# Product 7 of Strassen's scheme as a block product over two groups, in a matmul with RMSNorm

## The chip, the cores and the metric

The kernel runs on one core of one Trainium2 chip. The metric is the device time of an execution in microseconds; three runs of the kernel before gave 220.73 (median), 220.69 and 220.97. A core has TensorE (matmuls, into PSUM), VectorE, ScalarE and GpSimd (called POOL in the profile), and SyncE (SP), which here only issues DMAs. Each engine works through its own instructions in the order of the program; semaphores tie them together.

## The reference

```python
m, k, n = 2048, 2048, 2048          # all float32, eps = 1e-5
x = np.matmul(a, b)
rms = np.sqrt(np.mean(x ** 2, axis=-1, keepdims=True) + eps)
return gamma * x / rms
```

## The kernel before

The 2048 rows of `a` are 16 row blocks of 128 rows (`mb` 0 to 15). Blocks 0 to 3 are the head: their product runs while `b` streams in, partly as plain matmuls (L388). From then on the 2048x2048 matrix `b` stays in SBUF as bf16, in two halves `j` of N, each as eight tiles `raw[j][kp]`.

**Groups.** Blocks 4 to 15 are six groups `g` = 2 to 7 of two blocks, `ra` = 2g and `rb` = 2g+1. For a group and a half `j`, the 2x2 block product (two row blocks, two column chunks of 512, K taken as pairs of 128) is done by Strassen's seven products; each is eight matmuls of 128x128 by 128x512 into one PSUM bank (`product`, L289, matmul at L285). The sums of quarters of `b` were made in the head (`b_sums`, and `b_sums_in_place`, L273, which adds the diagonal quarters to the off-diagonal ones). The sums of quarters of `a` are five tiles `s_1`, `s_2`, `s_5`, `s_6`, `s_7` (`a_sums`, L254, each one 128x1024 fp16 operation on VectorE at L260), overwritten for each group. Product 7 is (a12 - a22), which is `s_7`, times the in-place quarter `b_quarter(j, kp, 1, 0)`.

**A half of a group** is `group_half` (L582). TensorE's order is products 2, 5, 1, 4, 3, 7, 6; products 4 and 3 add into the banks of 2 and 5 after those have been copied out. ScalarE copies banks into the x tiles (`c` at L597, `x21` at L608, `x12` at L613) and squares finished chunks with a running sum (`square`, L299; `last_squares`, L573, takes those that VectorE finished last). VectorE makes the differences and sums (L601, L605, L610, L615, L619, L624). The chunk `x22` also serves as scratch `t` and `c`, so it is the first x tile that a half writes (L597). PSUM has seven banks for this, in rotation.

**Work around it** is put in by hand at eight points of a half, `hooks` 0 to 7 (`hooks_of`, L634): point 1 lies after the first product, 2 after the second, 3 after product 1, 4 after product 4, 5 after product 3, 6 after product 7, 7 after product 6. In the first half (`j` = 0) of a group the two blocks of the next group are prepared: `row_norm` (L214, two squares on ScalarE at L219), `row_factor` (L225, four small VectorE operations), `row_apply` (L236: ScalarE scales the fp32 row block to fp16, L242) and `transpose_dma` (L194: SP issues a DMA transpose out of the fp16 rows, L195). The fp16 rows lie in two slots of `head_at` (`a16_slot`, L80). Also in the first half, block 2g-2 is scaled by gamma and 1/rms (`scale`, L363, on VectorE at L370) at point 3 and stored at point 4 (`store`, L374, SP at L376), behind the transpose that point 4 issues. In the second half, point 2 finishes block 2g-1 (`finish`, L378: scale and store of each half row), points 3, 6 and 7 make the next group's sums, and at point 0 POOL waits for the first half's `x22` (`wait_for`, L125, and `load_after`, L628) and then loads two row blocks (L121) into the two buffers `a32`.

**x tiles.** Each row block's result is two fp32 tiles of 128x1024; eight slots `x_slot` go round (`x_tile`, L313), four for a group.

**The last group** is `last_group` (L705), with its own order: products 5, 1, 4, 3, 7 for both halves, then 2 and 6, the very last in two quarters (L800), and the end of the normalization.

Of the kernel before, what the change touches and what calls it, by code (L numbers as in the profile page):

```python
# [17 lines left out]
def kernel(  # L18
# [21 lines left out]
    CH = 512  # L40
# [39 lines left out]
    def a16_slot(mb):  # L80
        if mb == HB:
            return gamma_sb[:, 0:HALF].bitcast(FP16)
        flat = head_at.rearrange("p t r m -> p (t r m)").bitcast(FP16)
        return flat[:, (2 + mb % 2) * K:(3 + mb % 2) * K]

    s_sum = {s: consts.tile([P, KP, P], FP16, name=f"s_{s}") for s in (1, 2, 5, 6, 7)}

    def at(mb):
# [161 lines left out]

    def sum_of(g, s):
        return s_sum[s].bitcast(BF16) if g < G0 else s_sum[s]

# [42 lines left out]
    x_half = {}  # L296
    n_x = [0]

# [7 lines left out]
    def square_half(mb, h):  # L306
# [4 lines left out]
                             scale=inv_sqrt_n, accum_out=msq[mb][:, c:c + 1])  # L311

    def x_tile(mb, h):  # L313


        if (mb, h) not in x_half:
            n = n_x[0]
            n_x[0] += 1
            if n < 8:
                slot = n  # L320
            else:
                g = n // 4
                slot = ((0, 4, 1, 5), (0, 1, 4, 5))[g // 2 % 2 == 0][n % 4] + 2 * (g % 2)
            x_half[mb, h] = x_slot[slot]
        return x_half[mb, h]
# [256 lines left out]
    def group_half(g, j, hooks):  # L582
# [21 lines left out]
        product(g, j, 1, p1)  # L604
        nc.vector.tensor_tensor(out=t, in0=p1, in1=t, op=ALU.subtract)  # L605
        at_hook(3)
        product(g, j, 4, p2, start=False)
        nc.scalar.copy(out=x21, in_=p2)  # L608
        square(rb, x21)
        nc.vector.tensor_tensor(out=x11, in0=t, in1=x21, op=ALU.add)  # L610
        at_hook(4)
# [4 lines left out]
        at_hook(5)  # L616
        p7 = new_bank()
        product(g, j, 7, p7)
        nc.vector.tensor_tensor(out=x11, in0=p7, in1=x11, op=ALU.add)  # L619
        late.append((ra, x11))  # L620
        at_hook(6)
# [3 lines left out]
        late.append((rb, x22))  # L625
        at_hook(7)

    def load_after(g, mb):  # L628
# [5 lines left out]
    def hooks_of(g, j):  # L634
# [13 lines left out]
        if j == 0:  # L648
            if g == G0:
                hook(0, finish, 0, (1,))  # L650
                hook(1, row_norm, nxt)
                hook(1, take_rms, 1)
                hook(2, pair_sub)
                hook(2, row_factor, nxt)
                hook(2, apply, nxt)
                hook(2, row_norm, nxt + 1)
                hook(2, pair_sums)
                hook(2, a_sums, g, (7, 6))
                hook(2, finish, 0, (0,))
                hook(2, finish, 1, (1,))  # L660
                hook(2, row_factor, nxt + 1)
                hook(2, pair_ends)
                hook(2, scale, 1, (0,))
                hook(4, apply, nxt + 1)
                hook(4, store, 1, (0,))
                hook(7, late.insert, 0, (r2, None))
            else:
                done = [2 * g - 2, 2 * g - 1]
                if g == G0 + 1:
                    done.insert(0, r3)  # L670
                else:
                    hook(1, row_norm, nxt)
                for mb in done:
                    hook(1, take_rms, mb)
                hook(2, row_factor, nxt)
                hook(2, apply, nxt)
                if g == G0 + 1:
                    hook(2, finish, r3)
                hook(2, row_norm, nxt + 1)
                hook(3, scale, 2 * g - 2)  # L680
                hook(3, row_factor, nxt + 1)
                hook(4, apply, nxt + 1)
                hook(4, store, 2 * g - 2)
        else:
# [4 lines left out]
            else:  # L689
                hook(2, finish, 2 * g - 1)  # L690
            if more:
                hook(3, a_sums, g + 1, (2, 5, 1))
                hook(6, a_sums, g + 1, (7,))
                hook(7, a_sums, g + 1, (6,))
# [10 lines left out]
    def last_group():  # L705
# [35 lines left out]
        for j in range(2):  # L741
# [3 lines left out]
            nc.scalar.copy(out=t[j], in_=p5)  # L745
            last_squares()
            product(g, j, 1, p1)
            add(t[j], p1, t[j], ALU.subtract)
            if j == 0:
                finish(2 * g - 2)  # L750
            product(g, j, 4, p4[j])
            nc.scalar.copy(out=x21[j], in_=p4[j])
            add(x11[j], t[j], x21[j])
            if j == 0:
                finish(2 * g - 1)
            product(g, j, 3, p5, start=False)
            nc.scalar.copy(out=x12[j], in_=p5)
            square(ra, x12[j])
            add(t[j], x11[j], x12[j])
            p7 = new_bank()  # L760
            product(g, j, 7, p7)
            add(x11[j], p7, x11[j])
            square(ra, x11[j])
            if j == 0:
                product(g, j, 2, p4[j], start=False)
                nc.scalar.copy(out=x21[j], in_=p4[j])
                square(rb, x21[j])
                seed = p7
                add(seed, t[j], x21[j], ALU.subtract)
# [5 lines left out]
        halves = [slice(0, CH // 2), slice(CH // 2, CH)]  # L775
        half = [bank[:, 0:CH // 2] for bank in (p1, p7)]
        for bank, col in zip(half, halves):
# [77 lines left out]
```

## Time and profile before

| | |
|---|---|
| median of three runs (lowest, highest) | 220.73 us (220.69, 220.97) |
| profiled execution: span, first to last instruction | 219.1 us; the runs' median is 1.6 us above it, for what lies around the span |
| TensorE matmul (PE) | 209.2 us busy, 95%, 1032 instructions |
| VectorE (DVE) | 165.9 us, 76%, 326 |
| ScalarE (ACT) | 127.0 us, 58%, 263 |
| GpSimd (POOL) | 36.4 us, 17%, 75 |
| granted TensorE clock over the span | 0.994 |
| matmuls of the groups (L285) | start at 41.20 us, without a pause from 66.73 us |
| stores to `out` | 29 of 512 KB, median 3.7 us from issue to landing |
| loads of row blocks | 10 of 1024 KB, median 9.0 us |
| DMA transposes of row blocks | 10, median 4.3 us |

How to read it: each engine's busy time is added up over the whole span. The profile gives, for each group of instructions, the source line, engine, operation, tiles, shapes and count, then busy time and the mean duration of one in ns, then the idle time of the engine just before them and what ended it. The chain that ended last is followed back from the last instruction; its shares tell which engine's work sets the end. In a timeline, each row is a start and a length in us, and the bracket at its end gives the idle time before and its releaser. "SPq" is SP's queue, "PEclk" the TensorE clock that was granted, as a fraction of full speed.

### The profile page before, as it was taken

How to read it: one execution, taken by the hardware profiler on the slowest of the kernel's cores; microseconds unless marked ns; L12 is line 12 of the kernel's file. 1: busy time of each engine (PE TensorE's matmuls, PEld its weight loads, DVE VectorE, ACT ScalarE, POOL GpSimd, SP SyncE). 2: the span in 40 equal slices, each digit the busy share in tenths (PEclk: the TensorE clock that was granted, in tenths of full speed). 3: DMA queues.
4: the chain of work that ended last, by engine and by line, in shares of the span. 5: the costliest groups of instructions: out<-in, count | busy, mean ns of one | idle time of the engine just before them, and what ended most of it. 6: DMA issues, size and time to landing. Idle time of an engine off the chain costs nothing.

```text
span 219.1 us, 3041 instructions
## 1 busy us (share of the span) xinstructions
PE 209.2 (95%) x1032; PEld 97.7 (45%) x1032; DVE 165.9 (76%) x326; ACT 127.0 (58%) x263; POOL 36.4 (17%) x75
## 2 busy tenths in 40 slices
PE   7799999999999999999999999999999999999970
PEld 3344544444455444444444444444444444444440
DVE  1128899999989998969696639946795759787771
ACT  2110002930599898588945996289747996334471
POOL 7554443433020002200110002000200000000040
PEclk9999999999999999999999999999999999999997
DMA  7999999999929698946799149955699259145045
GB/s 156 168 202 206 204 206 209 212 208 228 407 77 330 243 276 218 349 188 165 212 320 399 64 88 271 350 244 96 160 298 400 37 106 361 79 167 219 1 170 215
DMA packets 36720, 46.60 MB, mean 213 GB/s; under 512 B 22240, under 2 KB 26336, under 8 KB 35424
## 3 DMA queue, kind: packets, MB, share of 16 engines
q0 software_dynamic: 10608, 23.86, 44.1%
q1 hardware_dynamic: 25824, 22.29, 33.7%
q10 hardware_dynamic: 272, 0.26, 0.3%
q8 instruction: 8, 0.13, 0.2%
q14 instruction: 8, 0.07, 0.1%
HBM read 34.60 MB, written 16.78 MB: 234 GB/s over the span
## 4 chain that ended last, share of the span: by engine, by line
PE 92%; DMA 3%; ACT 1%; POOL 1%; issue 1%; DVE 0%; ACTq 0%; POOLq 0%
PE acc L285 71%; PE acc L388 16%; DMA early<-in_a_dram 3%; PE tbank L419 2%; PE tbank L168 2%; PE acc L800 1%; POOL b L102 0%; PE acc L185 0%; PE tbank L185 0%; ACT a L738 0%; DVE head_at L173 0%; ACTq L850 0%; ACT sq L803 0%; ACT rms L352 0%; POOL t_left masks.py:199 0%
## 5 line engine op out<-in xcount | busy, mean ns | idle before, releaser
L285 PE MATMUL acc<-b,s 128*128 128x512 bf16 x408 | 93.3, 379 | 0.0
L285 PEld LDWEIGHTS <-s 128*128 128x128 f16 (+1 forms) x512 | 50.0, 98 | 59.6 <-DVE s L260 0.2
L388 PE MATMUL acc<-b,head_at 128*128 128x512 bf16 x176 | 43.0, 379 | 1.2 <-DMA b<-in_b_dram 0.8
L303 ACT ACTIVATE sq<-x 128x512 bf16<-128x512 f32 x53 | 33.4, 630 | 6.9 <-DVE x L731 3.0
L370 DVE SCALAR_TENSOR_TENSOR x<-x,r,gamma_sb 128x1024 f32<-128x1024 f32 x28 | 34.9, 1282 | 0.7
L219 ACT ACTIVATE sq<-a 128x1024 bf16<-128x1024 f32 x24 | 25.3, 1054 | 3.2 <-DMA a<-in_a_dram 2.5
L388 PEld LDWEIGHTS <-head_at 128*128 128x128 bf16 x176 | 16.9, 97 | 20.4 <-issue 1.3
L242 ACT ACTIVATE head_at<-a,s 128x2048 f16<-128x2048 f32 x10 | 20.0, 1996 | 3.3 <-DVE s L229 3.3
L102 POOL DMA_DIRECT2D b<-in_b_dram x32 | 17.2, 541 | 20.6 <-DMA b<-in_b_dram 14.2
L430 ACT COPY x<-acc 128x512 f32<-128x512 f32 x5 | 2.9, 582 | 24.6 <-PE acc L388 24.6
L285 PEld LDWEIGHTS <-head_at 128*128 128x128 f16 (+1 forms) x112 | 10.9, 98 | 13.2
L285 PE MATMUL acc<-early,head_at 128*128 128x512 bf16 x64 | 14.5, 379 | 0.0
L285 PEld LDWEIGHTS <-at_even 128*128 128x128 f16 x96 | 9.4, 98 | 11.3
L285 PE MATMUL acc<-early,s 128*128 128x512 bf16 x56 | 14.2, 379 | 0.0
L260 DVE TENSOR_TENSOR s<-head_at 128x1024 f16<-128x1024 f16 (+5 forms) x22 | 13.4, 635 | 0.1
L615 DVE TENSOR_TENSOR x<-x,x 128x512 f32<-128x512 f32 x9 | 6.2, 693 | 8.8 <-ACT x L613 8.3
L127 POOL COPY pace<-x 128x1 f32<-128x1 f32 x4 | 1.7, 413 | 66.2 <-DVE x L624 64.9
L597 ACT COPY x<-acc 128x512 f32<-128x512 f32 x9 | 5.2, 573 | 11.5 <-PE acc L285 11.5
L173 DVE COPY head_at<-tbank 128x1024 bf16<-128x1024 bf16 x7 | 4.8, 692 | 8.6 <-PE tbank L168 8.5
L285 PE MATMUL acc<-t_left,s 128*128 128x512 bf16 x48 | 11.3, 379 | 0.0
L783 POOL TENSOR_SCALAR x<-x,r 128x512 f32<-128x512 f32 x1 | 2.7, 2657 | 51.2 <-DVE r L346 51.2
L276 DVE TENSOR_TENSOR b<-b 128x1024 bf16<-128x1024 bf16 x16 | 10.8, 686 | 0.2
(112 smaller groups left out, 238.0 us busy)
## 6 DMA issues: line engine op xcount, KB each, us to landing
out_dram<-x SPq DMA_DIRECT2D x29, 512.0 KB, 3.7
a<-in_a_dram POOLq DMA_DIRECT2D x10, 1024.0 KB, 9.0
b<-in_b_dram POOLq DMA_DIRECT2D x32, 256.0 KB, 10.0
a<-in_a_dram POOLq DMA_DIRECT2D x4, 512.0 KB, 9.8
early<-in_a_dram POOLq DMA_DIRECT2D x7, 256.0 KB, 10.0
gamma_sb<-in_gamma_dram POOLq DMA_DIRECT2D x2, 512.0 KB, 8.4
out_dram<-x SPq DMA_DIRECT2D x3, 256.0 KB, 2.6
out_dram<-a SPq DMA_DIRECT2D x1, 768.0 KB, 3.3
```

Of the source, the lines that this page charges most:

```text
L102: nc.gpsimd.dma_start(out=raw[j][kp][:, t, :], in_=b[lo:lo + P, j * HALF:(j + 1) * HALF])
L173: nc.vector.tensor_copy(out=head_at[:, 2 * kp:2 * kp + 2, :, :], in_=view)
L219: nc.scalar.activation(out=junk, in_=a32[mb][:, h * HALF:(h + 1) * HALF], func=ACTF.Square, scale=2.0 ** -8, accum_out=n2[:, h:h + 1])
L242: nc.scalar.activation(out=a16[mb], in_=a32.pop(mb), func=ACTF.Copy, scale=factor.pop(mb))
L260: nc.vector.tensor_tensor(out=sum_of(g, s)[:, lo:hi, :], in0=x[:, lo:hi, :], in1=y[:, lo:hi, :], op=op)
L276: nc.vector.tensor_tensor(out=flat[:, 1:3, :], in0=flat[:, 1:3, :], in1=flat[:, 0::3, :], op=ALU.add)
L285: nc.tensor.matmul(bank, lhsT[:, kp, :], rhs, start=(start and kp == 0), stop=(kp == KP - 1), skip_group_check=not start)
L303: nc.scalar.activation(out=sq[:, 0:CH], in_=src, func=ACTF.Square, scale=inv_sqrt_n, accum_out=msq[mb][:, c:c + 1])
L370: nc.vector.scalar_tensor_tensor(out=x, in0=x, scalar=inverse_of[mb], in1=gamma_sb[:, h * HALF:(h + 1) * HALF], op0=ALU.mult, op1=ALU.mult)
L388: nc.tensor.matmul(bank, head_at[:, kt, r, :], head_rhs(c, kt), start=(kt == 0), stop=(kt == KT - 1))
L597: nc.scalar.copy(out=c, in_=one[1])
L615: nc.vector.tensor_tensor(out=t, in0=t, in1=x12, op=ALU.add)
```

## The change

From group 4 on, two groups form a pair: 4 with 5, and 6 with 7. Product 7 of both groups and both halves of N is then one 2x2 block product: the rows are the two groups' `s_7`, the columns the two halves `j`, and K is cut in two halves of four `kp`. It is done by seven block products of four matmuls each, 28 matmuls in all for 4 x 8 = 32 before (`sevenths`).

- The first group of a pair leaves product 7 out of both halves, the second too. The seven parts run in three steps: `one` (parts 1 and 7) at point 6 of the first group's second half, `two` (parts 6, 2, 5, 4) at its point 7, `three` (part 3) at point 1 of the second group's first half. For the last group, step `three` follows its first product.
- The z sums, of quarters of `b`: four for each of four k, each 128x512 bf16 on VectorE, made once, in group 4: three for each k at points 4 to 7 of the first half, the fourth for all k at point 1 of the second. One is in place, two go to a region of `head_at`, and the fourth to `x_slot[3]`, which from then on holds no result rows.
- The y sums, of halves of the two groups' `s_7`: four operations of 128x512 fp16 on VectorE for each pair. They use `s_1` and half of `s_6` as room, so sums 1 and 6 of the second group are made in that group's own first half. The second group's `s_7` has a place of its own.
- Partial results pass from bank to bank by a ScalarE copy (`seed`), twice for a pair. The result chunks of the product are added to `x11` of both groups by VectorE; for the second group they are put there first (one by a ScalarE copy), and `t` and `x21` are added in two operations for one.
- The second group finishes block 2g-1 first and 2g-2 later, since 2g-2 is complete only after step `three`.
- The fp16 rows of blocks 6 to 15 are written in place, into the front half of their fp32 buffer `a32`.
- The x slots are a written-out table over the seven that are left.

```diff
     def a16_slot(mb):
         if mb == HB:
             return gamma_sb[:, 0:HALF].bitcast(FP16)
-        flat = head_at.rearrange("p t r m -> p (t r m)").bitcast(FP16)
-        return flat[:, (2 + mb % 2) * K:(3 + mb % 2) * K]
+        if mb == HB + 1:
+            return head_at.rearrange("p t r m -> p (t r m)").bitcast(FP16)[:, 3 * K:4 * K]
+        return a32[mb].bitcast(FP16)[:, 0:K]
...
+    z_sum = {3: z_store[:, 0], 2: z_store[:, 1],
+             4: x_slot[3].bitcast(BF16).rearrange("p (k n) -> p k n", k=KQ)}
+    s7_second = spare[1].bitcast(FP16).rearrange("p (k m) -> p k m", k=KP)
+    y_sum = {3: s_sum[1][:, 0:KQ], 2: s_sum[1][:, KQ:], 4: s_sum[6][:, 0:KQ]}
...
+    slot_of = {(r, h): r + HB * h for r in range(HB) for h in range(2)}
+
+    for n, slots in enumerate(((0, 4, 1, 5), (2, 6, 3, 7), (0, 1, 4, 5), (2, 7, 6, 1),
+                               (0, 5, 4, 2), (6, 1, 7, 5))):
+        for m, slot in enumerate(slots):
+            slot_of[HB + 2 * n + m % 2, m // 2] = slot
...
         nc.vector.tensor_tensor(out=t, in0=p1, in1=t, op=ALU.subtract)
+        if second_of_pair(g):
+            nc.vector.tensor_tensor(out=x11, in0=x11, in1=t, op=ALU.add)
         at_hook(3)
...
-        p7 = new_bank()
-        product(g, j, 7, p7)
-        nc.vector.tensor_tensor(out=x11, in0=p7, in1=x11, op=ALU.add)
-        late.append((ra, x11))
+        if g < FIRST_PAIR:
+            p7 = new_bank()
+            product(g, j, 7, p7)
...
+    def sevenths(g):
...
+        def one():
+            part(1, 1, y11, lambda k: z11[k], start=True)
+            part(7, 7, y_sum[3], lambda k: z_sum[3][:, k, :], start=True)
+            seed(2, 1)
+            nc.scalar.copy(out=to21, in_=b[7])
+
+        def two():
+            part(6, 2, y_sum[2], lambda k: z_sum[2][:, k, :])
+            part(2, 1, y12, lambda k: z21[k])
+            seed(3, 2)
+            add(to11, 1)
+            square(2 * g, to11)
+            part(5, 3, y21, lambda k: z12[k])
+            nc.vector.tensor_tensor(out=to22, in0=b[3], in1=to21, op=ALU.add)
+            part(4, 2, y22, lambda k: z_sum[4][:, k, :])
+            add(to21, 2)
+
+        def three():
+            part(3, 3, y_sum[4], lambda k: z22[k])
+            add(to12, 3)
+            square(2 * g, to12)
...
                 done = [2 * g - 2, 2 * g - 1]
+                if second_of_pair(g):
+                    done.reverse()
+                    hook(1, a_sums, g, (1,))
+                    hook(1, steps[g - 1][2])
+                    hook(2, a_sums, g, (6,))
...
+            if g == FIRST_PAIR:
+                for k in range(KQ):
+                    hook(1, z_sums, k, (3,))
+            if first_of_pair(g):
+                steps[g] = sevenths(g)
+                hook(3, a_sums, g + 1, (2, 5, 7))
+                hook(4, y_sums, g, (3, 1, 2))
+                hook(6, steps[g][0])
+                hook(7, y_sums, g, (4,))
+                hook(7, steps[g][1])
+            elif more:
                 hook(3, a_sums, g + 1, (2, 5, 1))
```

## The prediction

> **What bounds the kernel now.** I read the page's chain that ended last, then its costliest groups, then the chain in order of time.
>
> ```profile
> PE 92%; DMA 3%; ACT 1%; POOL 1%; issue 1%; DVE 0%; ACTq 0%; POOLq 0%
> ...
> L285 PE MATMUL acc<-b,s 128*128 128x512 bf16 x408 | 93.3, 379 | 0.0
> ```
> ```profile
> 66.73 143.74 PE acc L285 x666
> 210.47 1.76 PE acc L800 x16
> ```
>
> TensorE is the bound. From 66.73 us on it runs 666 matmuls with no idle time, 143.74 / 666 = 0.2158 us each. A group of two row blocks is 112 matmuls, 24.17 us; the first copy of group 4 starts at 117.27, some 0.07 us after its first eight matmuls, so group 4 starts at 115.47. Below, +x means x us after the start of its own group. VectorE (76% busy) and ScalarE (58%) cost nothing today because each runs a few us behind TensorE and seven PSUM banks cover that. The change makes TensorE read VectorE's results sooner, so next I read the timelines of VectorE, ScalarE and SP's queue in group 4 (start us, length us; what the engine waited for in brackets).
>
> ```profile
> 127.82 0.68 DVE L610 TENSOR_TENSOR x<-x 128x512 f32<-128x512 f32 x1
> 130.70 0.69 DVE L615 TENSOR_TENSOR x<-x,x 128x512 f32<-128x512 f32 x1 [2.20 <-ACT x L613]
> 131.31 0.68 DVE L619 TENSOR_TENSOR x<-acc,x 128x512 f32<-128x512 f32 x1
> 131.91 0.68 DVE L624 TENSOR_TENSOR x<-acc,x 128x512 f32<-128x512 f32 x1
> 132.51 0.68 DVE L601 TENSOR_TENSOR x<-acc,x 128x512 f32<-128x512 f32 x1
> ...
> 133.37 2.48 DVE L370 SCALAR_TENSOR_TENSOR x<-x,r,gamma_sb 128x1024 f32<-128x1024 f32 x2
> 135.77 0.68 DVE L605 TENSOR_TENSOR x<-acc,x 128x512 f32<-128x512 f32 x1
> 136.37 1.88 DVE L260 TENSOR_TENSOR s<-head_at 128x1024 f16<-128x1024 f16 x3
> 138.17 0.68 DVE L610 TENSOR_TENSOR x<-x 128x512 f32<-128x512 f32 x1
> ```
> ```profile
> 128.21 1.99 ACT L242 ACTIVATE head_at<-a,s 128x2048 f16<-128x2048 f32 x1
> 130.11 0.56 ACT L613 COPY x<-acc 128x512 f32<-128x512 f32 x1
> ...
> 131.33 0.57 ACT L597 COPY x<-acc 128x512 f32<-128x512 f32 x1
> ```
> ```profile
> 124.56 7.39 SPq L195 DMA_TRANSPOSE head_at<-head_at  x2
> 132.04 4.24 SPq L376 DMA_DIRECT2D out_dram<-x  x4
> ```
>
> The reader is to see how late these queues are. In the first half ScalarE does two row norms and two scalings to fp16 (L242) beside its copies, so the copy of product 3 (L613), over on TensorE at +10.36, comes at +14.64, and VectorE's L615 ends at +15.84. VectorE reaches the next group's sums (L260 x3), program point 3 of the second half, only at +20.9 (136.37 - 115.47). The store of row block 6, scaled by 125.93, leaves at 132.04 (+16.57): in SP's queue it stands behind the transpose of block 11, which waits for the second L242.
>
> **What goes.** Two pairs of groups, 28 matmuls for 32 in each: 8 x 0.2158 = 1.73 us off the path. Row: 0.2158 us each. The Trainium skill (TensorE: Matmul & The Clock Gate, Back-to-back issue gap) gives about 131 ns as the sustained roofline for such matmuls in a stream with weight loads; by that estimate the saving is 1.05 us. The trace decides.
>
> Group 4 now has 48 matmuls in its first half (10.36 us) and 72 in its second; group 5 has 52 and 48; groups 6 and 7 likewise.
>
> **What is added, and where it is late.** Steps of VectorE between starts, from the rows above: a 128x512 f32 operation 0.60, `finish` of a block 2.66 with its reciprocal, three sums 1.80. Sums of 128x512 in bf16 (L271): three start 1.00 apart, 0.335 each, and last 0.418. The new `z` and `y` sums have that size and two-byte type; I take 0.335, up to 0.418 where one needs the other's result.
>
> Part 7 of the new product reads y-sum 3. TensorE is there at +10.36 + 40 x 0.2158 + 4 x 0.2158 = +19.85. VectorE can't be, in any group of the kind: from +15.84 it has the sum with product 6 (0.60), L601 (0.60), `finish` (2.66), L605 (0.60), three sums (1.80), L610 (0.60) and the y-sum itself (0.42): +23.1.
>
> **Group 4** has the z sums too. The one after L610 in the first half is hidden: VectorE waits 2.20 us there. From +15.84: z sums of k=1 and k=2 (2.1), sum with product 6 to +18.6, k=3 to +19.65. The next four write into x slot 3, so they wait for the store of block 6's right half. It is issued second, at 133.31 (+17.84), and landed 6.6 us later, loads having been issued in the same moment (133.28); stores with no load behind them took 3.6, the one sent 1.24 us ahead of the loads 4.2. In the changed kernel the loads wait for the sum with product 6 and start at about +19.3, 1.4 us behind the store: I take 4.0, ends 3.6 and 6.6. So +21.85, then four z sums (1.35), L601 to +23.8, `finish` +26.45, L605 +27.05, three sums +28.85, L610 +29.45, y-sum +29.87. TensorE waits 10.05 us (19.85 to 29.9), 9.1 of it idle in one piece.
>
> What a piece costs beyond itself shows in the clock rows at the end of the span (window, length, busy time per engine, granted clock, DMA):
>
> ```profile
> 212.00:213.00 1.00, 0.22 (x3) 0.00 (x0) 0.65 (x2) 0.82 (x5) 0.37 (x1) 1.00 1.00 369
> ...
> 215.00:216.00 1.00, 0.00 (x0) 0.00 (x0) 0.00 (x0) 0.00 (x0) 0.00 (x0) 1.00 0.90 348
> 216.00:217.00 1.00, 0.00 (x0) 0.00 (x0) 0.00 (x0) 0.00 (x0) 0.00 (x0) 0.83 1.00 412
> 217.00:218.00 1.00, 0.00 (x0) 0.00 (x0) 0.00 (x0) 0.00 (x0) 0.00 (x0) 0.50 0.46 178
> ```
>
> The last matmul ended at 212.23; 0.83 over one us is half rate from 216.66, so the clock halves after 4.4 us without matmuls. The price of a cold start: the eight matmuls at the start (L147) begin 0.43 apart, so they cost 8 x 0.21 = 1.7 us more. I take 1.7 for each idle piece above 4.4; no row shows a restart after a pause, so the ends are 0 and 3.4. The Trainium skill (same page, What's actually happening) says that the activity window is 3.4 us long and free-running, so by it the pieces of 5.3 and 5.5 us below may or may not hold a whole idle window; the estimate is then up to 1.7 us less, in group 5, where the start is not hidden.
>
> Group 4: 10.05 + 1.7 = **+11.75**.
>
> **Group 5.** Only seven x slots are left, and block 11's right half takes slot 1, which is block 9's left half. Its first write is the copy of product 2 in the second half (L597), so that copy waits for the store of block 9, which stands in SP's queue behind block 13's transpose. ScalarE's chain is the one of group 4 plus one square less one square, L242 ending at about +14.9; the store leaves 1.93 later (130.11 to 132.04 in the rows), +16.83. The loads start 0.6 behind it: landing 4.4, between 4.2 (1.24 ahead) and the three that left with the loads (5.1, 6.2, 6.6). So the copy ends at +21.85 and product 4, which adds into the bank that it reads, starts at +21.9 for +16.4. That is 5.5 us idle, and 1.7 cold. Product 6 ends at +27.1 by warm matmuls; VectorE (L601 +22.5, `finish` +25.15, L605, the added sum, first sum +26.95) is just in time for group 6. **+7.2**.
>
> **Group 6.** The same trap with slot 2 (block 10, block 13's right half): store at +16.57, no loads now, landing 3.6 as at 180.39, copy to +20.8, product 4 at +20.8 for +15.54, cold. VectorE: L601 +21.45, `finish` +24.1, L605, sums +26.5, L610, y-sum +27.5. TensorE, cold, reaches part 7 at +26.85 and waits for that: 27.55 for 19.85. The cold start is hidden here. **+7.7**.
>
> **Group 7.** No product 7 in it, no L242; VectorE ends its sums near +18.7 where TensorE ends the last product 2 at +18.1, with product 6 of one half behind it as cover. +0.3; by the like rows from 191.57 to 209.5, 0 to 1.
>
> **Costed at nothing.** (a) Two seeds and a copy on ScalarE in each second half, 3 x 0.57 by L597: it waits there for TensorE anyway (3.84 us ahead of 141.44). The seed of bank 3 must fit into part 2, 0.86 us; without room 0.6 per pair. (b) Sums 1 and 6, moved into the next first half: ready at +1.3 for product 1 at +4.3. (c) Rows in place: a load now waits for the transpose out of its buffer. Block 11's landed at 130.26 + 4.3, +19.1; POOL gets there at +19.3, and the norms that read the load come over 10 us after it lands. In group 5 the second load waits to +19.4, with the same cover.
>
> **Sum**: 11.75 + 7.2 + 7.7 + 0.3 - 1.73 = +25.2. The profiled execution's span is 219.1; the median of the runs, 220.73, is 1.6 above it for what lies around. 219.1 + 25.2 + 1.6 = **245.9**.
>
> **Rivals.**
> 1. *The stores don't hold the copies* (they land early, or ScalarE is later than I think). For: 3.6 us landings exist. Against: SP's order in the rows. Then group 4 waits 7.8 (y-sum at +27.65) and 1.7 cold, group 5 0.65, group 6 3.3, group 7 0.3: 12.0 net, **232.8**.
> 2. *Restarts cost double*, 3.4 us twice in full and partly in group 6: **251**. For: nothing here shows how long the clock stays low after a pause. Against: eight slow matmuls at the start.
> 3. *The product fits*: y-sum 3 is ready by +19.85 and the saved matmuls show: 220.73 - 1.73 = **219.0**. It decides at VectorE's first sum (L260): that must start by 19.85 - 0.42 - 0.60 - 1.80 = +17.0. The row says +20.9, and its cause, ScalarE's two scalings, stays.
> 4. *The change doesn't do what it says* (a stage waits on a bank or a buffer that I missed): any time, mostly above.
>
> **Chances.** Forecast 0.68 (own range 240 to 253: landings -1.3 to +4.7, cold starts -3.4 to +3.4, z sums +0.7, not all at once); rival 1 0.14; rival 2 0.10; rival 3 0.03; rival 4 0.05. The range 235 to 253 leaves out rival 1's point, rival 3 and part of 4. A change under 0.2% (0.4 us), about what a measurement of this kernel can tell, has 0.01; faster 0.03; slower 0.96.
>
> **What would show it.** VectorE's y-sum (a 128x512 f16 sum) about 29.9, 27.5 us after the start of groups 4 and 6 with TensorE idle ahead of part 7; idle TensorE ahead of product 4 in the second half of groups 5 and 6, put down to L597's copy, and that to a store; PEclk under 1.0 in three places; about 25 us more of TensorE idle or at half clock. Wrong would be: L260 x3 near +17, copies that don't wait for stores, or a clock at 1.0 throughout.

## The result, and the profile after

| | before | after |
|---|---|---|
| median on the same chip (lowest, highest) | 220.85 us (220.69, 221.51) | 246.98 us (246.66, 248.88) |
| ratio, 95% interval | | 1.1189 [1.1148, 1.1231] |
| span of the profiled execution | 219.1 us | 245.2 us |
| granted TensorE clock over the span | 0.994 | 0.954 |

The change costs 12%. The forecast was 245.9. In the profiled executions the span grew by 26.1 us, where the forecast had 25.2.

Of the changed kernel's page: the engines' totals, the granted clock in 40 slices, the chain that ended last, and the group of matmuls that headed the list before.

```profile
PE 214.4 (87%) x1024; PEld 97.8 (40%) x1024; DVE 178.4 (73%) x354; ACT 130.2 (53%) x269; POOL 36.4 (15%) x75
...
PEclk9999999999999999999999779999599997999995
...
PE 9%; DVE 3%; ACT 1%; issue 1%; ACTq 0%; DVEq 0%
...
L305 PE MATMUL acc<-b,s 128*128 128x512 bf16 x344 | 80.0, 379 | 0.0
```

Eight matmuls fewer, 1024 for 1032, and yet PE is busy 5.2 us longer: the three dips of PEclk (slices 23 and 24, 29, and 34; the last slice is the end of the kernel in both) are matmuls at half rate. The chain, 92% PE before, can no longer be followed back: its shares add up to 14%. Where a chain breaks off early, the waits are the better view. These are TensorE's waits within the groups (line, releaser: us in total, times, longest). Lines have moved: L305 is the matmul of a product, L614 the copy of product 2 into scratch (L597 before), L618 the difference made from it (L601), L687 the matmul of a part, L662 the z sums, L675 the y sums.

```profile
PE acc L305 <- ACT x L614: 12.6, 3, 6.3
PE acc L305 <- DVE x L618: 5.3, 1, 5.3
PE acc L687 <- DVE s L675: 1.6, 2, 0.9
```

19.5 us of idle TensorE in six waits, none of which was there before. They lie in the second halves of groups 4, 5 and 6. The groups' first matmuls start at 115.60, 151.40 and 181.46 us. First group 4: VectorE's timeline (start, length), then TensorE's.

```profile
137.26 1.43 DVE L662 TENSOR_TENSOR x<-b,head_at 128x512 bf16<-128x512 bf16 x4 [1.26 <-DMA out_dram<-x]
138.61 0.68 DVE L618 TENSOR_TENSOR x<-acc,x 128x512 f32<-128x512 f32 x1
...
139.47 2.48 DVE L387 SCALAR_TENSOR_TENSOR x<-x,r,gamma_sb 128x1024 f32<-128x1024 f32 x2
141.87 0.68 DVE L622 TENSOR_TENSOR x<-acc,x 128x512 f32<-128x512 f32 x1
142.47 1.28 DVE L280 TENSOR_TENSOR s<-head_at 128x1024 f16<-128x1024 f16 x2
...
144.27 0.68 DVE L633 TENSOR_TENSOR x<-x 128x512 f32<-128x512 f32 x1
144.87 0.42 DVE L675 TENSOR_TENSOR s<-s,t_first 128x512 f16<-128x512 f16 x1
```
```profile
139.35 3.57 PE L305 MATMUL acc<-early,at_even 128*128 128x512 bf16 x8 [5.27 <-DVE x L618]
142.71 1.78 PE L687 MATMUL acc<-b,s 128*128 128x512 bf16 x4
145.34 1.04 PE L687 MATMUL acc<-head_at,s 128*128 128x512 bf16 x4 [0.85 <-DVE s L675]
```

The reader is to see one unbroken queue on VectorE: the four z sums wait for the store that frees x slot 3, and from then on everything up to the y-sum, ready at 145.29 (+29.7 from the group's start; forecast +29.87), runs back to back. TensorE meets that queue twice. The large wait is ahead of product 3, whose eight matmuls (x8) add into product 5's bank, and L618 reads that bank; only 0.85 us is left ahead of part 7. Product 3 took 3.57 us for eight matmuls, where eight take 1.89 at full clock.

In group 5 the chain is a store, a copy and a product. SP's queue, then ScalarE, then TensorE:

```profile
168.51 9.39 SPq L393 DMA_DIRECT2D out_dram<-x  x4
```
```profile
173.65 0.58 ACT L614 COPY x<-acc 128x512 f32<-128x512 f32 x1 [5.76 <-DMA out_dram<-x]
```
```profile
174.28 4.00 PE L305 MATMUL acc<-early,head_at 128*128 128x512 bf16 x9 [6.32 <-ACT x L614]
```

The store of block 9 leaves behind a transpose, at +17.1; the copy into its slot starts when it has landed, 5.1 us later, and product 4 follows the copy. In group 6 the same three rows are at 198.12, 201.87 and 202.50, a wait of 5.35 us, and then 0.71 ahead of part 7.

The clock, in windows of 2 us (start and end, length, busy time per engine, granted clock, DMA share, GB/s):

```profile
136.00:138.00 2.00, 0.00 (x0) 0.00 (x0) 0.74 (x3) 0.75 (x3) 0.55 (x2) 0.85 0.50 170
...
144.00:146.00 2.00, 1.15 (x5) 0.31 (x4) 1.93 (x5) 0.87 (x3) 0.00 (x0) 0.94 0.80 328
...
170.00:172.00 2.00, 0.00 (x0) 0.00 (x0) 0.00 (x0) 0.00 (x0) 0.47 (x1) 0.88 1.38 326
172.00:174.00 2.00, 0.00 (x0) 0.00 (x0) 0.00 (x0) 0.35 (x1) 0.06 (x1) 0.50 0.73 178
...
178.00:180.00 2.00, 2.00 (x10) 0.88 (x9) 1.97 (x5) 1.27 (x4) 0.00 (x0) 0.91 1.01 422
```

0.85 over 2 us is full rate until 137.4 and half after it; read in the same way, the clock is at half from 137.4 to 144.2 and from 171.5 to 178.4 (and, in group 6, from 202.2 to 205.7). It drops 3.3, 3.6 and 5.1 us after the last matmul (134.1, 168.0, 197.2) and stays low for another 3.2 to 4.9 us after TensorE has resumed.

### The profile page after: what moved, and what is told of

It reads as the page before. It is cut to its first block, busy times and chain, and to the rows that moved or that the text cites. A ratio compares the mean times of both kernels' runs of the same rounds, so it can differ in the third digit from the quotient of the medians.

```text
span 245.2 us, 3060 instructions
## 1 busy us (share of the span) xinstructions
PE 214.4 (87%) x1024; PEld 97.8 (40%) x1024; DVE 178.4 (73%) x354; ACT 130.2 (53%) x269; POOL 36.4 (15%) x75
## 5 line engine op out<-in xcount | busy, mean ns | idle before, releaser
L305 PE MATMUL acc<-b,s 128*128 128x512 bf16 x344 | 80.0, 379 | 0.0
L305 PEld LDWEIGHTS <-s 128*128 128x128 f16 (+1 forms) x448 | 43.6, 98 | 52.2 <-DVE s L280 0.6
L237 ACT ACTIVATE sq<-a 128x1024 bf16<-128x1024 f32 x24 | 25.3, 1053 | 3.6 <-DMA a<-in_a_dram 3.0
L305 PE MATMUL acc<-early,at_even 128*128 128x512 bf16 x48 | 14.2, 458 | 11.5 <-ACT x L614 6.2
L305 PE MATMUL acc<-early,head_at 128*128 128x512 bf16 x64 | 16.5, 416 | 6.3 <-ACT x L614 6.3
L260 ACT ACTIVATE a<-a,s 128x2048 f16<-128x2048 f32 x10 | 20.0, 1998 | 3.4 <-DVE s L247 3.3
L305 PEld LDWEIGHTS <-at_even 128*128 128x128 f16 x96 | 10.1, 105 | 25.5 <-issue 16.1
L305 PEld LDWEIGHTS <-head_at 128*128 128x128 f16 (+1 forms) x112 | 11.4, 102 | 21.2 <-issue 9.3
L614 ACT COPY x<-acc 128x512 f32<-128x512 f32 x9 | 5.2, 576 | 18.0 <-DMA out_dram<-x 10.1
L305 PE MATMUL acc<-early,s 128*128 128x512 bf16 x56 | 14.2, 379 | 0.0
L618 DVE TENSOR_TENSOR x<-acc,x 128x512 f32<-128x512 f32 x9 | 6.2, 688 | 10.8 <-ACT x L614 9.8
L280 DVE TENSOR_TENSOR s<-head_at 128x1024 f16<-128x1024 f16 (+5 forms) x20 | 12.2, 629 | 0.1
L305 PE MATMUL acc<-t_left,s 128*128 128x512 bf16 x48 | 11.3, 379 | 0.0
```

Of the source, the lines that this page charges most:

```text
L237: nc.scalar.activation(out=junk, in_=a32[mb][:, h * HALF:(h + 1) * HALF], func=ACTF.Square, scale=2.0 ** -8, accum_out=n2[:, h:h + 1])
L260: nc.scalar.activation(out=a16[mb], in_=a32.pop(mb), func=ACTF.Copy, scale=factor.pop(mb))
L280: nc.vector.tensor_tensor(out=sum_of(g, s)[:, lo:hi, :], in0=x[:, lo:hi, :], in1=y[:, lo:hi, :], op=op)
L305: nc.tensor.matmul(bank, lhsT[:, kp, :], rhs, start=(start and kp == 0), stop=(kp == KP - 1), skip_group_check=not start)
L614: nc.scalar.copy(out=c, in_=one[1])
L618: nc.vector.tensor_tensor(out=t, in0=two[1], in1=c, op=ALU.add)
```

## The experiments

The theory: three causes, which meet in the second halves: (A) stores that stand behind a transpose in SP's queue hold x slots that the change made scarcer; (B) the y sum stands too late in VectorE's program; (C) the clock halves in the pauses. The rivals: that the restart at half clock is the main price, or the fp16 rows in place, which make loads wait.

### Store ahead of the second transpose

```diff
                 hook(3, scale, done[-2])
+                if g >= FIRST_PAIR:
+                    hook(3, store, done[-2])
                 hook(3, row_factor, nxt + 1)
                 hook(4, apply, nxt + 1)
-                hook(4, store, done[-2])
+                if g < FIRST_PAIR:
+                    hook(4, store, done[-2])
```

> Edit to the changed kernel: from group 4 on, the store of the first finished block leaves at point 3, ahead of the second transpose in SP's queue, and not behind it. Theory (the stores hold the copies of product 2 in groups 5 and 6, by the reused x slots 1 and 2): group 5 loses its wait of 6.3 us and the 2.0 us of cold clock behind it (minus 0.6 that VectorE's first sum then sets), group 6 keeps only the wait for y-sum 3, some 4.3 us less, group 4 starts its last four z sums 1.3 us sooner: 247.0 - 7.7 - 4.3 - 1.3 = 233.7 us. Rival (ScalarE is late by its own work, the store only ends last by chance): the copies come 1 us sooner at most, 244 to 247 us.

Measured: 235.59 us (234.14 to 236.38), ratio 1.0653 [1.0610, 1.0696]; span 232.3, 12.9 less than after's. SP's queue in group 5 of this kernel, then TensorE's waits in it:

```profile
161.99 1.35 SPq L393 DMA_DIRECT2D out_dram<-x  x2
165.30 2.07 SPq L213 DMA_TRANSPOSE at_even<-a  x1
```
```profile
PE acc L687 <- DVE s L675: 4.1, 2, 2.4
PE acc L305 <- DVE x L618: 3.9, 1, 3.9
PE acc L305 <- ACT x L614: 2.7, 3, 1.4
```

The store now leaves 3.3 us ahead of the transpose, and the copies no longer wait for it: L614's total falls from 12.6 to 2.7. The median is 1.9 us above the 233.7 expected, far below the rival's 244. What is uncovered is VectorE's lateness: the waits for the y sum rise from 1.6 to 4.1. (A) is shown: half of the loss, with the restarts that it brings about, is one place in one queue.

### The y sum ahead of `finish`

```diff
-            else:
+            elif not first_of_pair(g):
                 hook(2, finish, 2 * g - 2 if second_of_pair(g) else 2 * g - 1)
...
-                hook(3, a_sums, g + 1, (2, 5, 7))
-                hook(4, y_sums, g, (3, 1, 2))
+                hook(3, a_sums, g + 1, (7,))
+                hook(3, y_sums, g, (3,))
+                hook(3, finish, 2 * g - 1)
+                hook(4, y_sums, g, (1, 2))
...
+                        hook(4, z_sums, k, (3,))
+                hook(5, a_sums, g + 1, (2, 5))
```

> Edit to the changed kernel, the stores as they are: in the second half of groups 4 and 6 VectorE makes the sum 7 of the next group and y-sum 3 ahead of the scaling of block 2g-1, and the last four z sums and sums 2 and 5 after that. Theory (two causes of about equal weight, y-sum 3 behind VectorE's other work in groups 4 and 6, stores in groups 5 and 6): group 4 gets part 7 some 6 us sooner, group 6 only 0.7, since its product 4 still waits for a copy behind a store, group 5 nothing: 240.3 us; up to 3 us of it may be lost where the store of block 7, now later, holds the result chunk that takes its slot. Rival (the stores are the whole cause): 246 to 247. Rival (y-sum 3 is the whole cause): both groups lose their waits, 234 or less.

Measured: 242.16 us (240.47 to 242.94), ratio 1.0946 [1.0892, 1.1001]; span 239.9. TensorE in group 4 of this kernel:

```profile
136.48 3.57 PE L305 MATMUL acc<-early,at_even 128*128 128x512 bf16 x8 [2.57 <-DVE x L618]
139.85 1.06 PE L687 MATMUL acc<-b,s 128*128 128x512 bf16 x4
140.75 1.03 PE L687 MATMUL acc<-head_at,s 128*128 128x512 bf16 x4
```

No wait is left ahead of part 7 in either group; product 4 still waits 6.28 and 5.35 us for the copies in groups 5 and 6. Counted from the group's start, part 7 begins 4.4 us sooner in group 4 (+25.3 for +29.7; some 6 were expected, but product 3 still waits 2.57) and 0.8 us sooner in group 6: where a store holds the group up anyway, an earlier y sum brings little. (B) is shown, at 5.3 us by itself, for VectorE's order as a whole. The edit moves the four z sums too, from ahead of L618 to behind the y sum, and the wait for L618 falls from 5.27 to 2.57 us; no run separates the two moves.

### Both orders together

> store_first and y_first together, on the changed kernel. Theory (two separate causes): no wait for a store and none ahead of part 7; against store_first (span 232.3 us) group 4 gets part 7 some 3.2 us sooner and group 6 2.4 us sooner: span 226.7, time 228.5 us. What is left above the kernel before is VectorE's late reading of product 5's bank in group 4 (2.6 us and a cold start of 1.7), 0.9 us in front of product 4 in groups 4 and 6, and the end. Rival (a third wait comes in where the first two go): 231 us or more.

Its edit is the two above. Measured: 229.93 us (229.56 to 230.39), ratio 1.0405 [1.0388, 1.0422]; span 227.4, 17.8 less than after's. The two alone give 12.9 + 5.3 = 18.2, so they add up nearly. The granted clock over the span is 0.993. Group 4 of this kernel, the same wait as in the kernel above:

```profile
136.74 1.89 PE L305 MATMUL acc<-early,at_even 128*128 128x512 bf16 x8 [2.57 <-DVE x L618]
```

Six waits are left, 7.2 us in all, of which 2.57 is this one. No copy waits for a store any more, no matmul of the groups runs at half rate, and part 7 waits no more. Five of the six are VectorE's and ScalarE's own lateness. The sixth, 1.14 us ahead of part 6 in group 6 for its y sum, goes back to a DMA transpose: sum 7 of the next group, with which that stretch of VectorE's queue begins, waits for it.

```profile
188.84 0.69 DVE L280 TENSOR_TENSOR t_first<-head_at 128x1024 f16<-128x1024 f16 x1 [1.31 <-DMA head_at<-a]
```

### Two slots of group 6 exchanged

```diff
-                               (0, 5, 4, 2), (6, 1, 7, 5))):
+                               (0, 5, 2, 4), (6, 1, 7, 5))):
```

> The changed kernel with two slots exchanged in the table: block 13's right half takes slot 4 (block 8's right half, stored a group earlier) and block 12's right half slot 2 (block 10's left half); the stores stay behind the transposes. Theory (it is the slot that joins the copy of product 2 to the late store): in group 6 product 4 no longer waits 5.35 us, y-sum 3 comes as in store_first's group 6, 4.3 us sooner; group 5 keeps its 6.3 us, since its slot is as it was: 242.7 us. Rival (the late store delays group 6 in another way, by SP's queue or by traffic): 246 to 247.

Measured: 244.64 us (243.85 to 245.42), ratio 1.1066 [1.1037, 1.1095]; span 242.0. Of TensorE's timeline in group 6:

```profile
197.54 3.61 PE L305 MATMUL acc<-early,at_even 128*128 128x512 bf16 x16 [0.91 <-ACT x L614]
...
204.44 1.67 PE L687 MATMUL acc<-head_at,s 128*128 128x512 bf16 x4 [2.42 <-DVE s L675]
```

The scratch tile of the second half is now a slot that came free long before: that wait falls from 5.35 to 0.91 us, group 5's, which has its own slots, stays at 6.30. The span gives 3.2 us and not 4.3, since the next wait, for the y sum, grows from 0.71 to 2.42. It was the slot.

### The pauses filled with matmuls

```diff
+    def keep_warm(n):
+        bank = ps_t.tile([P, CH], FP32, name="tbank")
+        for i in range(n):
+            nc.tensor.matmul(bank, identity, b_quarter(0, 0, 0, 0), start=(i == 0),
+                             stop=(i == n - 1))
...
+        if j == 1 and g in (FIRST_PAIR + 1, FIRST_PAIR + 2):
+            keep_warm(16)
         product(g, j, 4, p2, start=False)
...
+        if j == 1 and g == FIRST_PAIR:
+            keep_warm(16)
         product(g, j, 3, p5, start=False)
```

These matmuls have no reader. They fill some 3.5 us of each pause and leave its cause as it is.

> The changed kernel with 16 more matmuls, whose result goes nowhere, ahead of product 4 in the second half of groups 5 and 6 and ahead of product 3 in that of group 4, where TensorE waits for 5.3 to 6.3 us; they take 3.5 us of the wait and keep the pauses under 3 us. Theory (the clock halves in these pauses; it costs time on the path only in group 5, since in groups 4 and 6 the slow matmuls end before y-sum 3 is ready): the granted clock stays at 1.0 and group 5 loses 2.0 us: 245.0 us. Rival (the cold starts cost on the path in all three): 241.5 us. Rival (the clock isn't on the path): 247.0.

Measured: 247.72 us (246.30 to 248.87), ratio 1.1207 [1.1159, 1.1254], no different from after. As a test of (C) it missed, because the clock dropped all the same in what was left of the pauses. Two windows of group 5, in which matmuls stop at 172.45 and resume at 175.09:

```profile
172.00:174.00 2.00, 0.44 (x3) 0.10 (x1) 0.00 (x0) 0.00 (x0) 0.53 (x1) 1.00 1.20 201
174.00:176.00 2.00, 0.91 (x3) 0.34 (x3) 0.89 (x3) 1.51 (x4) 0.00 (x0) 0.76 0.84 303
```

A pause of 2.65 us was enough: half rate from 175.04, the moment at which work resumed, and sixteen matmuls took 5.26 us for 3.61. The second kernel fills nearly all of each pause: 22 matmuls ahead of product 3 in group 4, 26 and 22 ahead of product 4 in groups 5 and 6, 14 and 8 ahead of part 7.

> As warm, but with so many idle matmuls that no pause of TensorE is over 1.2 us: 26 and 22 ahead of product 4 in groups 5 and 6, 22 ahead of product 3 in group 4, 14 and 8 ahead of part 7. In warm the clock still halved, after pauses of 3.25 and 2.65 us, so that run tells nothing of the price. Theory (a cold start costs time on the path only in group 5): clock 1.0 throughout, 2.0 us less than the changed kernel, 245.0 us. Rival (cold starts on the path in all three groups): 241.5. Rival (not on the path): 247.0.

Measured: 245.13 us (245.06 to 245.26), ratio 1.1092 [1.1076, 1.1109]; clock 0.994 over the span, as before the change. Group 5:

```profile
166.00:170.00 4.00, 4.00 (x21) 1.79 (x19) 1.38 (x2) 1.44 (x4) 0.72 (x2) 1.00 0.73 142
170.00:174.00 4.00, 3.30 (x16) 1.44 (x15) 0.16 (x1) 0.78 (x2) 0.53 (x1) 1.00 1.04 264
174.00:178.00 4.00, 4.00 (x20) 1.81 (x19) 3.93 (x6) 2.95 (x8) 0.00 (x0) 1.00 0.99 408
```

With the clock at 1.00 throughout, 1.9 us of 26 are gone. The trace shows where: from product 1 of one group to product 1 of the next, group 5 takes 27.27 us for after's 29.20, group 4 36.70 for 36.66 and group 6 33.43 for 32.97. So the cold restarts cost on the path in group 5 alone; in groups 4 and 6 TensorE waits for VectorE in that time. That the restart is the main price is refuted.

### The fp16 rows in place, alone

The kernel before, with only `a16_slot` changed:

```diff
-        flat = head_at.rearrange("p t r m -> p (t r m)").bitcast(FP16)
-        return flat[:, (2 + mb % 2) * K:(3 + mb % 2) * K]
+        if mb == HB + 1:
+            return head_at.rearrange("p t r m -> p (t r m)").bitcast(FP16)[:, 3 * K:4 * K]
+        return a32[mb].bitcast(FP16)[:, 0:K]
```

> The kernel before with one part of the change alone: the fp16 rows of blocks 6 to 15 are written in place. Theory: nothing waits for the buffers any longer than before, 220.8 us, within 0.3. Rival (the loads, which now wait for the transposes, come late): 221.5 to 224 us.

Measured: 221.04 us (220.79 to 221.63) beside 221.01, ratio 1.0003 [0.9989, 1.0018]. This part is free, and no cause.

### Can the saved matmuls be had?

Five versions, each put together from what the one before it showed. The first (`tuned`) has the stores first, sum 7, the y sums and sum 2 ahead of `finish`, the z sums spread over free places, squares put off, and half of block 8's `finish` moved into group 6:

```diff
-                    for k in range(KQ):
-                        hook(4 + k, z_sums, k, (0, 1, 2))
+                    hook(1, z_sums, 0, (0, 1, 2))
+                    hook(4, z_sums, 1, (2,))
+                    hook(4, z_sums, 2, (0, 1, 2))
+                    hook(6, z_sums, 3, (0, 1, 2))
...
-                hook(3, a_sums, g + 1, (2, 5, 7))
-                hook(4, y_sums, g, (3, 1, 2))
+                hook(3, a_sums, g + 1, (7,))
+                hook(3, y_sums, g, (3, 1, 2))
+                hook(3, a_sums, g + 1, (2,))
+                hook(3, finish, 2 * g - 1)
...
+                hook(4, a_sums, g + 1, (5,))
```

> The change with its side work put where the traces show room: stores ahead of the transposes; in groups 4 and 6 sum 7, the y sums and sum 2 ahead of the scaling of block 2g-1; z sums in VectorE's waits for the norms and for product 3's copy; two squares of a first half after the copy of the second half; half of block 8 scaled in group 6; in the last group block 13 scaled ahead of product 1's subtraction. Theory (the saving of 1.73 us is real and the rest is order): TensorE waits about 1 us in group 4 (VectorE is short there by its z sums) and 0.2 to 0.5 in the others: 220.0 to 221.5 us, about the time of the kernel before. Rival (VectorE hasn't the time for the 30 more operations wherever they stand): 224 us or more.

Measured: 223.98 us (223.52 to 224.82), ratio 1.0128 [1.0111, 1.0145]. The order wins back 23 of the 26 us. The expectation was missed, and the rival's 224 is about met: 1.8 us of waits remain ahead of parts that add into banks which VectorE's result sums (L716 there) have yet to read, and 1.9 us at four other places.

The second puts off sum 5 and the two sums that finish product 6 behind those reads:

```diff
-                hook(4, a_sums, g + 1, (5,))
+                pending.append(lambda: a_sums(g + 1, (5,)))
...
             nc.vector.tensor_tensor(out=to22, in0=b[3], in1=to21, op=ALU.add)
+            while pending:
+                pending.pop(0)()
```

> tuned with five places mended that its trace shows: the results of parts 1 and 5 taken out ahead of sum 5 and of the two operations that finish product 6 of that half (tuned waited 1.41 and 0.37 us for bank 3 there, and 0.36 for sum 1); the z sums of k=3 behind the reading of product 5's bank (0.62); half of block 8 scaled in VectorE's wait for the norm, so that no store stands before the transposes at that point (0.76 and 0.18). Theory (order alone stood in the way of the saving): TensorE waits some 0.8 us in groups 4 to 7 for tuned's 3.7: 221.1 us, at 220.4 to 221.6 level with the kernel before. Rival (VectorE's 28 more operations come out somewhere else): 222.5 or more.

Measured: 223.83 us (223.49 to 225.86), ratio 1.0120 [1.0082, 1.0159]: a miss, in the rival's range. The waits at the banks fell from 1.8 to 0.3, but the last group's product 5 now waited 0.9 for its sum, and the copies of product 2 (L615 there) held TensorE for 1.9.

The third takes the slots of group 6 from above, makes sum 5 of the last group early again, starts a row norm of the second group of a pair sooner and folds one product with gamma:

```diff
-                               (0, 5, 4, 2), (6, 1, 7, 5))):
+                               (0, 5, 2, 4), (6, 1, 7, 5))):
...
-                    hook(1, row_norm, nxt)
+                    hook(0 if second_of_pair(g) else 1, row_norm, nxt)
```

> tuned2 with four places mended that its trace shows: the slots of slot_g6 (1.18 us ahead of product 4 in group 6), sum 5 of the last group made ahead of the put-off operations, since that group begins with product 5 (0.88), the first row norm of group 5 ahead of ScalarE's copy (0.59 ahead of its product 4, ScalarE being 3 us later there than in group 4), and one gamma product of the last group taken into the scaling (0.45 at the end). Theory (order alone): 223.8 - 3.1 = 220.7 us, level with the kernel before. Rival (VectorE and ScalarE have no room in these groups, and what is taken away at one place comes back at the next): 222.5 or more.

Measured: 222.44 us (222.04 to 223.19), ratio 1.0064 [1.0046, 1.0082]. Better by 1.4 us, still slower than before the change, and short of the 220.7 expected.

The fourth makes sum 1 early, puts block 10's store behind the transpose again and the fourth z sums earlier:

```diff
-                if g >= FIRST_PAIR:
+                if g in (FIRST_PAIR, FIRST_PAIR + 1):
                     hook(3, store, done[-2])
...
-                    hook(1, a_sums, g, (1,))
...
-                        hook(4, z_sums, k, (3,))
+                        hook(3, z_sums, k, (3,))
+                pending.append(lambda: a_sums(g + 1, (1,)))
```

> tuned3 with the waits of TensorE that its trace still shows (some 2.5 us in groups 4 to 7) taken one by one: sum 1 of the second group made first of the put-off operations (0.38 and 0.80), the store of block 10 behind the transpose again, since no copy waits for its slot any more and the transpose lands later beside it (0.6 of the 0.75 ahead of part 7 in group 6), the last four z sums one operation sooner (0.28). Theory (the 1.73 us of eight matmuls are there to be had): 220.4 us, 0.1 to 0.4% under the kernel before. Rival (each wait comes back elsewhere): 222 us or more.

Measured: 221.65 us (220.87 to 224.64), ratio 1.0022 [0.9999, 1.0046]: level, where 220.4 was expected. In its trace 0.3 us of waits is left in the groups, and the last matmul ends at 211.42, before the change at 212.22. But the last store is issued at 214.78, before the change at 214.71. The windows of group 7 show why, in this kernel and then in the kernel before (PE, PEld, DVE, ACT, POOL busy):

```profile
200.00:205.00 5.00, 5.00 (x25) 2.27 (x24) 4.59 (x8) 4.25 (x11) 0.00 (x0) 1.00 0.43 170
205.00:210.00 5.00, 4.95 (x26) 2.48 (x26) 4.69 (x10) 2.89 (x8) 0.38 (x1) 1.00 0.11 45
```
```profile
200.00:205.00 5.00, 5.00 (x25) 2.29 (x24) 3.59 (x7) 2.98 (x7) 0.00 (x0) 1.00 0.25 97
205.00:210.00 5.00, 5.00 (x25) 2.25 (x24) 3.25 (x8) 2.68 (x7) 0.29 (x1) 1.00 0.00 0
```

VectorE is busy 9.3 of these 10 us, for 6.8 before: the sums that the change added and the work that was put off end here. The normalization then follows VectorE, and ScalarE behind it, and not TensorE. ScalarE's last square, in this kernel and then in the kernel before, starts 0.7 us and 0.1 us after the last matmul has ended:

```profile
212.11 0.38 ACT L960 ACTIVATE sq<-acc 128x256 bf16<-128x256 f32 x1
```
```profile
212.32 0.38 ACT L803 ACTIVATE sq<-acc 128x256 bf16<-128x256 f32 x1
```

The fifth is to give VectorE room: a half of one product with gamma goes to GpSimd, and block 13's rms is taken ahead of step `three`.

```diff
+                take_rms(2 * g - 1)
                 steps[g - 1][2]()
...
-                add(xa, xa, gam_left, ALU.mult)
+                add(xa[:, 0:CH], xa[:, 0:CH], gam[0], ALU.mult)
+                nc.gpsimd.tensor_tensor(out=xa[:, CH:], in0=xa[:, CH:], in1=gam[1], op=ALU.mult)
```

> tuned4 with two operations moved in the last group, where its trace shows VectorE without a pause from the start of the group to the end: block 13's root is taken ahead of step three's square on ScalarE (VectorE waits 0.88 us for it), and gamma times one chunk goes to GpSimd (0.6 us of VectorE). tuned4's TensorE ends 0.8 us sooner than the kernel before's, but its last store leaves 3.4 us behind the last matmul and not 2.5. Theory (VectorE's lateness in the last group eats the rest of the saving): some 0.9 us less, 220.5 us, 0.2 to 0.4% under the kernel before. Rival (the end hangs on ScalarE's squares and the store): 221.2 to 221.6, level as tuned4.

Measured: 221.23 us (220.61 to 223.35) beside 221.11, ratio 1.0006 [0.9986, 1.0027]: level again, where 220.5 was expected; the rival, that the end hangs on ScalarE's squares and the store, had 221.2 to 221.6. In its trace the last store leaves 3.1 us behind the last matmul, for 3.4 in the fourth version and 2.5 in the kernel before. The product given to GpSimd relieved VectorE by nothing (the last section shows why), so this run doesn't settle which of the two engines holds the end. No version that was run beats the kernel before.

## Why the prediction was right, point by point

Its mechanism held: the y sum late on VectorE, two stores behind transposes, the clock in the pauses. That the sum came within 1 us is in part luck: group 4 was put 1.9 us too high, group 5 and the end together 2.2 us too low. A group's length is read from the starts of its first matmuls.

| step | forecast | measured | what the runs showed |
|---|---|---|---|
| eight matmuls fewer | -1.73 | -1.73 | 24 matmuls from 190.09 to 195.27: 0.2158 each, as before |
| group 4 | +11.75 | +9.9 (35.80 for 25.9) | y-sum at +29.7 for +29.87; the restart was hidden |
| group 5 | +7.2 | +8.5 (30.06 for 21.6) | copy ends at +22.83 for +21.85; restart 2.0 for 1.7 |
| group 6 | +7.7 | +7.9 (33.82 for 25.9) | part 7 at +27.77 for +27.55 |
| group 7 and the end | +0.3 | +1.2 | 0.2 in the group, 1.0 after the last matmul |
| start, until group 4 | 0 | +0.3 | first matmul at 115.60 for 115.34 |
| sum | +25.2 | +26.1 | |

**Group 4** had the right y sum and the wrong place for the wait. The forecast has "TensorE waits 10.05 us (19.85 to 29.9), 9.1 of it idle in one piece", ahead of part 7, and 1.7 of restart added. It left out product 3, which adds into product 5's bank and so needs L618, and a wait of 0.90 us ahead of product 4 for ScalarE's copy. In that order the half-rate matmuls (product 3 and part 1) ran while the y sum was still on its way: they took the place of waiting, and the 1.7 fell out. The kernel with the pauses filled says the same, since only group 5's restart could be won. The four z sums waited for the store as forecast, until +21.7 for +21.85. Two of the prediction's readings are off and change little: by the matmul rows group 4 of the kernel before starts at 115.34 and not at 115.47, and product 3, which it has over at +10.36, is over at +8.6 (40 matmuls), so ScalarE's copy is later behind TensorE than it says.

**Group 5** was mis-sized in two terms. The store left at +17.1 for +16.83, and the copy began 5.1 us after it, where 4.4 was taken; so the copy ended 1.0 later. And sixteen matmuls from the restart took 5.45 us for 3.45, 2.0 more, where 1.7 was taken.

**Group 6** came within 0.2, **group 7** within its bounds. **The end** was forecast with no cost of its own. The last reciprocal comes 1.9 us after the last matmul (239.13 after 237.24), 0.9 before the change (213.15 after 212.22): ScalarE's squares of the last quarters stand behind the square of the chunk before, at 237.03, and ScalarE is late there because block 14's reciprocal comes only 1.7 us ahead of the last matmul's end (235.51), 2.8 ahead before the change (209.45).

**Costed at nothing** held for the rows in place (1.0003) and for the two seeds, 0.57 us each, and sums 1 and 6, which no wait of TensorE names.

**The rivals.** Stores that don't hold the copies were built: 235.59 us, for which rival 1 had 232.8; group 4 waits there 3.9 at product 3 and 1.7 ahead of part 7. In groups 4, 5 and 6 the matmuls after the pause took 2.4, 2.0 and 1.5 us longer than at full rate, not 3.4, and only group 5's were on the path. The 4.4 us without matmuls after which the prediction has the clock halve, read at the end of the span, is no threshold: the last section shows a pause of 2.57 us that halves it. That the product fits was off by all of the waits: even with nothing in VectorE's way but its own work, product 3 still waited 2.57 us.

The Trainium skill (TensorE: Matmul & The Clock Gate, Back-to-back issue gap) gives 131 ns as the sustained figure for matmuls of this size; the row of 0.2158 above decides against it here.

## What to carry to other kernels

Before matmuls are removed by adding sums, read for each new operand how far behind TensorE the engine is that will make it, at that very point of its queue: here VectorE was several us late at a time when it was idle a quarter of the span. Follow the buffer too: a slot that is reused sooner ties a copy to a store, and a store to whatever stands ahead of it in its queue, a transpose for another group included. And price the saving against the busiest stretch of the engine that pays for it: a new order of the work won back the 26 us lost, and of the 1.73 us of TensorE that the change saves the fourth version had 0.8 left at its last matmul and none at its last store, where VectorE was busy for 9.3 of 10 us.

## What the runs showed of the hardware

- **The clock moves on a fixed grid.** The changes at 137.4, 144.2, 171.5, 178.4, 202.2 and 205.7 us are 6.8, 27.3, 6.9, 23.8 and 3.5 apart: 2, 8, 2, 7 and 1 steps of 3.41. What counts is how a pause lies on it. A pause of 2.57 us ahead of product 3 halved the clock in the kernel with the y sum first (eight matmuls in 3.57 us) and not in the kernel with both orders (1.89). In the first, nearly all of it lies in one step: matmuls ran for 0.85 us of the 3.41 that end at 136.50, where the clock drops. In the second, whose one change of the clock is at 224.30, steps counted back from there meet at 135.55 and cut the pause (134.17 to 136.74) in two, with 1.9 and 2.2 us of matmuls in the two steps. In the kernel with 16 filling matmuls a pause of 2.65 us halved it, with 0.8 us of matmuls in the 3.41 that end at 175.04: a pause may leave a step a quarter busy and still cost the clock. The Trainium skill (TensorE: Matmul & The Clock Gate, What's actually happening) has a free-running window of 3413 ns, which the grid confirms, and asks for an idle window, which these pauses were not.
- **GpSimd held VectorE up.** In the last version, VectorE and then GpSimd:

```profile
205.18 1.57 DVE L887 TENSOR_TENSOR x<-x,gamma_sb 128x512 f32<-128x512 f32 x1
```
```profile
204.42 1.78 POOL L931 TENSOR_TENSOR x<-x,gamma_sb 128x512 f32<-128x512 f32 x1 [41.48 <-DVE x L887]
```

  VectorE's 128x512 multiplication takes 1.57 us for the usual 0.69, and ends 0.55 after GpSimd's: by half the work given away nothing was won, since both halves by VectorE took 1.22 in the version before. The Trainium skill (SBUF — State Buffer, SBUF: two separate sides) says that VectorE, with two inputs in SBUF, and GpSimd lock a pair of ports for a whole instruction; these two rows agree with that.
